# Two-layer product with GELU: W1 and W2 loaded in longer rows, and another order of the first two blocks

## The chip, the cores and the metric

The kernel runs on one core of a Trainium2 chip. The metric is the device time of one execution in microseconds (us), as a median over several runs. One more execution was recorded by the hardware profiler, and all durations below come from that one.

## The reference

```python
batch, m, k, h, n = 16, 512, 768, 3072, 768     # all float32
y = np.matmul(x, w1) + b1
y = 0.5 * y * (1.0 + erf(y / np.sqrt(2.0)))     # GELU
return np.matmul(y, w2).astype(np.float32)
```

x has 8192 rows in all. The kernel multiplies in 16-bit floats and adds up in 32 bits.

## The kernel before

**Seven products instead of eight.** The kernel takes the 8192 rows in eight blocks of 1024. In every block a matrix product is cut into two by two quarters, and the eight products of quarters are replaced by seven products of sums of quarters (the Winograd form of Strassen's method). The sums on the weight side are called T1 to T4, the raw quarters B11, B12, B21, B22; those on the x side are made by `x_sums` (L295), those on the hidden side by `g_sum`.

**First product.** A unit (`Unit1`) computes 128 hidden columns of the left half of W1 and 128 of the right half, for the two 512-row halves of the block: seven products `p1` to `p7` of three 128x512 matmuls each (L363). Twelve units make a block. Each unit needs one tile of W1: four raw quarters of 384 elements a partition, loaded and cast to 16 bits by GpSimd's DMA queue (`load_wt`, L186, DMAs on L195), and three more made of them by VectorE (`prep_wt`, L208; its operations are all recorded as L163). B12 is overwritten by T1. The finished tile of seven is also stored to DRAM by SyncE (`keep`, L205) for the blocks from 2 on.

**Second product.** For blocks 0 and 1 a unit (`Unit2`) computes 128 rows of each 512-row half with the same seven products, of twelve 128x384 matmuls each (L403). Blocks 2 to 7 use a second level of the method (`Unit3`, L455) on quarters of W2 which `split_w2` makes and stores to DRAM (L233) while blocks 0 and 1 run. The raw ones are stored as they lie; the computed ones pass through five staging buffers.

**Order.** The order on each engine is written out by hand. In a period (`period`, L577) TensorE does p1 of unit i, p7 of the unit j before it, p5 of i, p3 of j, p6 of i, p4 of j, p2 of i. Three PSUM steps hang on this: after p6 the sum is copied from bank bY to bank bZ (VectorE L570 or ACT L568), and p3 goes on there; p7 can only follow when that copy is done; VectorE then makes the two 32-bit sums c22 (L528) and c12 (L555), and ACT the GELU. Between the products `fill` puts VectorE's other work into the queues, by a budget in nanoseconds (`sums`), and DMAs at fixed points. Since engines work through their queues in order, an operation that waits for a transfer holds all that is queued behind it.

**The stretch around the change.** `seq` lists the 24 units of the first product of blocks 0 and 1; a unit's place in it is called its position. Block 0 goes first; block 1's x is loaded by GpSimd (`load_x`), transposed by SyncE's DMA queue (L283) into the layout the matmuls need, and summed on VectorE at the two positions ahead of block 1's first unit. Six slots hold W1 tiles: three of their own, three in the space of W2. A tile from number 6 on is loaded one position after block 1 has used the tile that lies in its slot. W2 is loaded (L214) in sixteen pieces of rows of 192 elements. At the turn from the first to the second product (`turn` in `period`) p1 of the first `Unit2` is spread between the last products of the last `Unit1`.

Of the kernel before, what the change touches and what calls it, by code (L numbers as in the profile page):

```python
# [10 lines left out]
P = 128  # L11
# [6 lines left out]
B11, B21, T1, B22, T3, T2, T4 = range(7)  # L18


@with_exitstack
def kernel(
# [24 lines left out]
    w2r = w2.rearrange("(hc p) n -> p hc n", p=P)  # L47
# [9 lines left out]
    w1s = [dp.tile([P, 7, KQ, P], F16, name=f"w1s{n}") for n in range(NH)]  # L57
# [56 lines left out]
    def wt_at(off):  # L114
        return cut(off, WT_N, "p (s k c) -> p s k c", s=7, k=KQ)
# [3 lines left out]
    wt_far = [wt_at(o_w2 + k * WT_N) for k in range(3)]  # L119
# [12 lines left out]
    def tmp_at(off):  # L132
# [8 lines left out]
    w2v = {slot: cut(off, W2_N, "p (h c n) -> p h c n", h=2, c=NH)  # L141
           for slot, off in ((B11, o_w2), (T3, o_w2 + W2_N), (T1, o_w2 + 2 * W2_N),
                             (B22, o_w2 + 3 * W2_N), (T2, o_x0),
                             (B21, o_x0 + W2_N + 2 * GS_N), (T4, o_x1 + XT_N))}
# [13 lines left out]
    with tc.manual_schedule():  # L158
# [27 lines left out]
        def load_wt(n):  # L186
            hi = hi_of(n)
            if n >= NH:
                wts[n] = wt_late[n % 4]
                nc.sync.dma_start(out=wts[n], in_=w1s[hi][:])  # L190
                return
            wts[n] = wt = wt_far[n - 3] if 3 <= n < 6 else wt_own[n % 3]
            for half in range(2):
                c0 = (half * NH + hi) * P
                nc.gpsimd.dma_start(  # L195
                    out=wt[:, 2 * half:2 * half + 2, :, :].rearrange("p a k c -> p (a k) c"),
                    in_=w1r[:, :, c0:c0 + P])

        def t_ops(o, n, q, ks=(0, 1, 2, 3)):

            for k in ks:
                d, a, b = ((T3, B22, T1), (T1, T1, B11), (T2, B22, T1), (T4, B21, T2))[k]
                later(n, lambda d=d, a=a, b=b: tt(o(d), o(a), o(b), SUB), q)
# [4 lines left out]
        def prep_wt(n):  # L208
            wt = wts[n]
            t_ops(lambda s: wt[:, s, :, :], KQ * P, soon)  # L210

        def load_w2(q, h, c):
            slot, r0, n0 = ((B11, 0, 0), (B21, NH, 0), (T1, 0, N2), (B22, NH, N2))[q]
            nc.gpsimd.dma_start(out=w2v[slot][:, h, c:c + NQ, :],  # L214
                                in_=w2r[:, r0 + c:r0 + c + NQ, n0 + h * N4:n0 + (h + 1) * N4])

        w2_parts = [(h, c) for c in (0, NQ) for h in range(2)]

        def prep_w2(h, c, q, ks):
            t_ops(lambda s: w2v[s][:, h, c:c + NQ, :], NQ * N4, q, ks)  # L220
# [125 lines left out]
        class Unit1:  # L346
# [11 lines left out]
            def mm(self, p, dst, first, c0, c1):  # L358
# [3 lines left out]
                for c in range(c0, c1):  # L362
                    nc.tensor.matmul(out=dst[:, 0:RH], lhsT=self.wt[:, slot, c, :],  # L363
# [13 lines left out]
            def right_done(self):  # L377
                hi = self.hi
                nc.scalar.activation(out=self.G[1][:, hi, :, :], in_=self.tmp, func=GELU,  # L379
                                     bias=b1t[:, NH + hi:NH + hi + 1])  # L380

            def left_done(self, row, bank):
                hi = self.hi
                nc.scalar.activation(out=self.G[0][:, hi, row, :], in_=bank[:, 0:RH], func=GELU,  # L384
                                     bias=b1t[:, hi:hi + 1])
# [175 lines left out]
        def p6(u):  # L561
            u.mm(6, bY[u.g % 2], False, 0, u.C)
            on_act = isinstance(u, Unit3) or (isinstance(u, Unit1) and u.sb > 0 and u.g % 2)
# [13 lines left out]
        def period(i, j, fill):  # L577

            turn = isinstance(j, Unit1) and not isinstance(i, Unit1)
            if turn and isinstance(i, Unit3):  # L580
# [16 lines left out]
            if turn:  # L597
                p7(j)
                fill(0)
                p1(i, 0, 5)  # L600
                p3(j)
                j.right_done()
                fill(0)
                p1(i, 5, 8)
                p4(j)
                p1(i, 8, i.C)
                copy_xy(i)
            else:
                if i and i.g:
                    p1(i, 0, i.C)  # L610
                    copy_xy(i)
                if j:
                    p7(j)
# [4 lines left out]
            if j and not turn:  # L618
# [4 lines left out]
            if j and not turn:  # L623
                j.right_done()
            fill(4)
            if j and not turn:
# [8 lines left out]
        wf = cut(GR + 8 * K, 8 * KQ * P).bitcast(FP32).rearrange(  # L635
            "p (h a c) -> p h a c", h=2, a=2 * KQ)
# [49 lines left out]
        for t in range(4, 8):  # L686
            if t == 6:
# [249 lines left out]
```

## Time and profile before

| | us |
|---|---|
| median of three runs | 882.42 |
| the three runs | 882.73, 877.61, 882.42 |
| the profiled execution | 877.73 |
| its span, first to last instruction | 876.0 |
| TensorE busy | 856.2 |
| VectorE busy | 650.2 |
| blocks 0 and 1, to the end of their second product | 248 |

A line of the timeline gives the start and the length in us, the engine, the line of the code, the operation, what it writes and reads, the shapes, how many were merged, and in brackets how long the engine stood idle before it and what it waited for. A line of the chain of waits gives start, length and what the execution was waiting on. A line of a DMA queue gives packets, MB and the time that the packets took as a share of the sixteen engines; a packet here is one row of a transfer, and times of packets overlap.

### The profile page before, as it was taken

How to read it: one execution, taken by the hardware profiler on the slowest of the kernel's cores; microseconds unless marked ns; L12 is line 12 of the kernel's file. 1: busy time of each engine (PE TensorE's matmuls, PEld its weight loads, DVE VectorE, ACT ScalarE, POOL GpSimd, SP SyncE). 2: the span in 40 equal slices, each digit the busy share in tenths (PEclk: the TensorE clock that was granted, in tenths of full speed). 3: DMA queues.
4: the chain of work that ended last, by engine and by line, in shares of the span. 5: the costliest groups of instructions: out<-in, count | busy, mean ns of one | idle time of the engine just before them, and what ended most of it. 6: DMA issues, size and time to landing. Idle time of an engine off the chain costs nothing.

```text
span 876.0 us, 16242 instructions
## 1 busy us (share of the span) xinstructions
PE 856.2 (98%) x6298; PEld 560.0 (64%) x6298; DVE 650.2 (74%) x1110; ACT 421.6 (48%) x686; POOL 95.4 (11%) x149
## 2 busy tenths in 40 slices
PE   8799999999999999999999999999999999999997
PEld 3344445666544599447984489744995459944697
DVE  5564577665546899578995799767997679956997
ACT  4577673111157712775128741477225771267511
POOL 6222210001100000200011000200002000010000
PEclk9999999999999999999999999999999999999999
DMA  9999683839969699996989969898898979967397
GB/s 215 177 268 187 108 174 118 327 146 243 243 200 299 180 320 346 255 292 198 325 323 263 291 224 321 291 287 208 286 329 278 309 168 309 350 225 262 104 295 275
DMA packets 155889, 219.42 MB, mean 250 GB/s; under 512 B 83532, under 2 KB 95236, under 8 KB 155812
## 3 DMA queue, kind: packets, MB, share of 16 engines
q1 hardware_dynamic: 112640, 181.01, 65.1%
q0 software_dynamic: 43136, 37.36, 23.0%
q8 instruction: 49, 0.80, 0.4%
q14 instruction: 28, 0.23, 0.1%
q10 hardware_dynamic: 36, 0.01, 0.0%
HBM read 180.30 MB, written 47.87 MB: 260 GB/s over the span
## 4 chain that ended last, share of the span: by engine, by line
PE 74%; DVE 13%; DMA 6%; issue 5%; POOL 1%; ACT 1%; SPq 0%; DVEq 0%; POOLq 0%; ACTq 0%
PE bY L363 17%; PE bX L363 11%; PE bY L455 10%; DVE arena L163 8%; PE bW L363 6%; PE bX L455 6%; PE bY L403 5%; PE bZ L363 5%; PE bX L403 4%; PE bZ L455 4%; PE bW L455 3%; DMA arena<-w1s 2%; PE bZ L403 2%; PE bW L403 2%; DMA arena<-in_w_dram 2%
## 5 line engine op out<-in xcount | busy, mean ns | idle before, releaser
L163 DVE TENSOR_TENSOR arena<-arena 128x768 f16<-128x768 f16 (+4 forms) x630 | 395.1, 656 | 18.6 <-DMA arena<-arena 8.0
L363 PEld LDWEIGHTS <-arena 128*128 128x128 f16 x2016 | 196.3, 98 | 245.1 <-issue 14.9
L455 PEld LDWEIGHTS <-arena 128*128 128x128 f16 x3528 | 292.1, 98 | 13.0 <-issue 4.5
L363 PE MATMUL bY<-arena 128*128 128x512 f16 x864 | 219.8, 380 | 7.9 <-DVE bZ L570 6.6
L528 DVE TENSOR_TENSOR arena<-bY,arena 128x512 f32<-128x512 f32 (+1 forms) x104 | 70.8, 681 | 160.1 <-PE bY L363 104.0
L363 PE MATMUL bX<-arena 128*128 128x512 f16 x576 | 141.8, 379 | 1.0 <-DMA arena<-w1s 1.0
L455 PE MATMUL bY<-arena 128*128 128x192 f16 x1512 | 139.8, 246 | 2.4 <-DVE bZ L565 2.4
L521 ACT COPY bY<-bX 128x512 f32<-128x512 f32 (+1 forms) x146 | 80.4, 550 | 127.5 <-DVE arena L497 90.8
L379 ACT ACTIVATE arena<-arena,b1t 128x1024 f16<-128x1024 f32 x96 | 110.3, 1149 | 60.5 <-DVE arena L555 60.5
L540 ACT COPY arena<-bW 128x512 f32<-128x512 f32 (+1 forms) x146 | 80.8, 553 | 93.4 <-PE bW L455 44.2
L403 PEld LDWEIGHTS <-arena 128*128 128x128 f16 x672 | 65.7, 98 | 44.2
L455 PE MATMUL bX<-arena 128*128 128x192 f16 x1008 | 92.0, 246 | 0.4
L555 DVE TENSOR_TENSOR arena<-bZ,arena 128x512 f32<-128x512 f32 (+1 forms) x104 | 70.5, 678 | 22.0 <-PE bZ L363 15.6
L363 PE MATMUL bW<-arena 128*128 128x512 f16 x288 | 78.5, 382 | 0.9 <-DVE arena L163 0.9
L363 PE MATMUL bZ<-arena 128*128 128x512 f16 x288 | 78.5, 382 | 0.0
L480 POOL DMA_DIRECT2D out_dram<-arena x42 | 30.1, 718 | 397.3 <-DVE arena L551 363.0
L384 ACT ACTIVATE arena<-bX,b1t 128x512 f16<-128x512 f32 x96 | 65.4, 681 | 7.9 <-PE bX L363 7.9
L384 ACT ACTIVATE arena<-bY,b1t 128x512 f16<-128x512 f32 x96 | 64.7, 674 | 0.0
L277 POOL DMA_DIRECT2D arena<-in_x_dram x60 | 32.4, 546 | 274.1 <-DMA arena<-arena 192.6
L568 ACT COPY bZ<-bY 128x512 f32<-128x512 f32 (+1 forms) x54 | 29.6, 548 | 52.9 <-DVE arena L555 36.3
L403 PE MATMUL bY<-arena 128*128 128x384 f16 x288 | 49.6, 326 | 0.0
L455 PE MATMUL bW<-arena 128*128 128x192 f16 x504 | 49.0, 246 | 0.1
(41 smaller groups left out, 359.7 us busy)
## 6 DMA issues: line engine op xcount, KB each, us to landing
arena<-w2s SPq DMA_DIRECT2D x294, 288.0 KB, 4.7
arena<-w1s SPq DMA_DIRECT2D x72, 672.0 KB, 6.5
out_dram<-arena POOLq DMA_DIRECT2D x42, 384.0 KB, 4.8
w2s<-arena SPq DMA_DIRECT2D x49, 288.0 KB, 3.9
arena<-in_x_dram POOLq DMA_DIRECT2D x60, 192.0 KB, 6.9
w1s<-arena SPq DMA_DIRECT2D x12, 672.0 KB, 5.2
out_dram<-arena SPq DMA_DIRECT2D x21, 384.0 KB, 3.2
arena<-in_w_dram POOLq DMA_DIRECT2D x16, 288.0 KB, 8.0
```

The source lines that it names most:

```text
L163: nc.vector.tensor_tensor(out=o, in0=a, in1=b, op=op)
L277: nc.gpsimd.dma_start(out=xhs[t], in_=xr[:, sb * 8 + t, :])
L363: nc.tensor.matmul(out=dst[:, 0:RH], lhsT=self.wt[:, slot, c, :], rhs=a[:, c, :], start=first and c == 0, stop=c == self.C - 1, skip_group ...
L379: nc.scalar.activation(out=self.G[1][:, hi, :, :], in_=self.tmp, func=GELU, bias=b1t[:, NH + hi:NH + hi + 1])
L384: nc.scalar.activation(out=self.G[0][:, hi, row, :], in_=bank[:, 0:RH], func=GELU, bias=b1t[:, hi:hi + 1])
L403: nc.tensor.matmul(out=dst[:, 0:N2], lhsT=a, rhs=w[:, :, c, :], start=first and c == 0, stop=c == self.C - 1, skip_group_check=True)
L455: nc.tensor.matmul(out=dst[:, t * N4:(t + 1) * N4], lhsT=a, rhs=w[:, c, :], start=first and c == 0 and t == 0, stop=c == NQ - 1, skip_grou ...
L480: eng.dma_start(out=orr[:, s0:s0 + 2, right * N2:(right + 1) * N2], in_=self.dst[:, r].rearrange("p t h n -> p t (h n)"))
L521: nc.scalar.copy(out=bY[u.g % 2][:, 0:u.F], in_=bX[u.g % 2][:, 0:u.F])
L528: nc.vector.tensor_tensor(out=u.c22(), in0=bY[u.g % 2][:, 0:u.F], in1=w[:, 0:u.F], op=ADD)
L540: nc.scalar.copy(out=w[:, 0:u.F], in_=bW[:, 0:u.F])
L555: nc.vector.tensor_tensor(out=u.c12(), in0=bZ[:, 0:u.F], in1=w[:, 0:u.F], op=ADD)
```

## The change

Unit k now takes columns 256k to 256k+127 as its left and 256k+128 to 256k+255 as its right part: the halves of W1 are made of alternating chunks of 128, and the rows of W2 and the bias are taken in the same alternation. A W1 tile is then one DMA of 1 KB rows, where it was two of 512 B rows. In the tile the four raw quarters lie interleaved (`w1_op` picks one out). W2 is loaded in nine DMAs of whole 3 KB rows, so B11 lies beside B12, and B21 beside B22; T1 gets a place of its own, and VectorE makes the sums three chunks at a time (`prep_w2`). There are seven slots for tiles. The list of units changes: seven of block 0 first, and the last of block 0 at position 17 instead of 20, six ahead of the end. The bZ copies of block 1 all go to VectorE (`sb >= ONE`, and ONE is 2). The special turn is removed.

```diff
 B11, B21, T1, B22, T3, T2, T4 = range(7)
+RAW = {B11: (0, 0), T1: (0, 1), B21: (1, 0), B22: (1, 1)}
...
     w1r = w1.rearrange("(kc p) c -> p kc c", p=P)
-    w2r = w2.rearrange("(hc p) n -> p hc n", p=P)
+    w2r = w2.rearrange("(hc s p) n -> p s hc n", s=2, p=P)
...
-    w1s = [dp.tile([P, 7, KQ, P], F16, name=f"w1s{n}") for n in range(NH)]
+    w1s = [dp.tile([P, 7 * KQ * P], F16, name=f"w1s{n}") for n in range(NH)]
     w2s = {(p, q): dp.tile([P, NQ, N4], F16, name=f"w2s{p}{q}")
...
     def wt_at(off):
-        return cut(off, WT_N, "p (s k c) -> p s k c", s=7, k=KQ)
+        return cut(off, WT_N)
+    def w1_raw(wt):
+        return wt[:, 0:4 * KQ * P].rearrange("p (k c) -> p k c", c=2 * P)
+    def w1_op(wt, slot):
+        raw = wt[:, 0:4 * KQ * P].rearrange("p (a k b c) -> p a b k c", a=2, k=KQ, b=2)
+        if slot in RAW:
+            return raw[:, RAW[slot][0], RAW[slot][1]]
+        return wt[:, slot * KQ * P:(slot + 1) * KQ * P].rearrange("p (k c) -> p k c", c=P)
...
     wt_own = [wt_at(o_wt + k * WT_N) for k in range(3)]
-    wt_far = [wt_at(o_w2 + k * WT_N) for k in range(3)]
+    W2P = 2 * W2_N
+    o_far = [o_w2 + W2P, o_w2 + W2P + WT_N, o_w2 + W2P + 2 * WT_N, o_w2 + W2P - WT_N]
+    slots = dict(enumerate([wt_at(o_wt + k * WT_N) for k in range(3)] + [wt_at(o) for o in o_far]))
+    slots.update({7: slots[0], 8: slots[1], 9: slots[2], 10: slots[3], 11: slots[4]})
     wt_late = [wt_at(o_wt2), wt_at(o_wt2 + WT_N)] + wt_own[:2]
...
              for k in range((o_x0 - o_stage) // WB)]
-    w2v = {slot: cut(off, W2_N, "p (h c n) -> p h c n", h=2, c=NH)
-           for slot, off in ((B11, o_w2), (T3, o_w2 + W2_N), (T1, o_w2 + 2 * W2_N),
-                             (B22, o_w2 + 3 * W2_N), (T2, o_x0),
-                             (B21, o_x0 + W2_N + 2 * GS_N), (T4, o_x1 + XT_N))}
+    w2rows = [cut(o_w2 + k * W2P, W2P, "p (c n) -> p c n", c=NH) for k in range(2)]
+    w2v = {}
+    for k, pair in enumerate(((B11, T3), (B21, B22))):
+        for m, slot in enumerate(pair):
+            w2v[slot] = w2rows[k][:, :, m * N2:(m + 1) * N2].rearrange("p c (h n) -> p h c n", h=2)
+    for slot, off in ((T2, o_x0), (T1, o_x0 + W2_N + 2 * GS_N), (T4, o_x1 + XT_N)):
+        w2v[slot] = cut(off, W2_N, "p (h c n) -> p h c n", h=2, c=NH)
     GS = [cut(o, GS_N, "p (c r) -> p c r", c=NH)
...
                 return
-            wts[n] = wt = wt_far[n - 3] if 3 <= n < 6 else wt_own[n % 3]
-            for half in range(2):
-                c0 = (half * NH + hi) * P
-                nc.gpsimd.dma_start(
-                    out=wt[:, 2 * half:2 * half + 2, :, :].rearrange("p a k c -> p (a k) c"),
-                    in_=w1r[:, :, c0:c0 + P])
-        def t_ops(o, n, q, ks=(0, 1, 2, 3)):
-            for k in ks:
-                d, a, b = ((T3, B22, T1), (T1, T1, B11), (T2, B22, T1), (T4, B21, T2))[k]
-                later(n, lambda d=d, a=a, b=b: tt(o(d), o(a), o(b), SUB), q)
+            wts[n] = slots[n]
+            nc.gpsimd.dma_start(out=w1_raw(wts[n]), in_=w1r[:, :, 2 * hi * P:2 * (hi + 1) * P])
...
         def prep_wt(n):
-            wt = wts[n]
-            t_ops(lambda s: wt[:, s, :, :], KQ * P, soon)
-        def load_w2(q, h, c):
-            slot, r0, n0 = ((B11, 0, 0), (B21, NH, 0), (T1, 0, N2), (B22, NH, N2))[q]
-            nc.gpsimd.dma_start(out=w2v[slot][:, h, c:c + NQ, :],
-                                in_=w2r[:, r0 + c:r0 + c + NQ, n0 + h * N4:n0 + (h + 1) * N4])
-        w2_parts = [(h, c) for c in (0, NQ) for h in range(2)]
-        def prep_w2(h, c, q, ks):
-            t_ops(lambda s: w2v[s][:, h, c:c + NQ, :], NQ * N4, q, ks)
+            o = {s: w1_op(wts[n], s) for s in range(7)}
+            for d, a, b in ((T3, B22, T1), (T1, T1, B11), (T2, B22, T1), (T4, B21, T2)):
+                later(KQ * P, lambda d=d, a=a, b=b: tt(o[d], o[a], o[b], SUB), soon)
+        def load_w2(k, c0, c1):
+            nc.gpsimd.dma_start(out=w2rows[k][:, c0:c1, :], in_=w2r[:, k, c0:c1, :])
+        W2C = 3
+        def prep_w2(d, c, q):
+            a, b = {T1: (T3, B11), T2: (B22, T1), T3: (B22, T3), T4: (B21, T2)}[d]
+            o = [w2v[s][:, :, c:c + W2C, :] for s in (d, a, b)]
+            later(2 * W2C * N4, lambda: tt(*o, SUB), q)
...
                 for c in range(c0, c1):
-                    nc.tensor.matmul(out=dst[:, 0:RH], lhsT=self.wt[:, slot, c, :],
+                    nc.tensor.matmul(out=dst[:, 0:RH], lhsT=w1_op(self.wt, slot)[:, c, :],
                                      rhs=a[:, c, :], start=first and c == 0,
...
                 nc.scalar.activation(out=self.G[1][:, hi, :, :], in_=self.tmp, func=GELU,
-                                     bias=b1t[:, NH + hi:NH + hi + 1])
+                                     bias=b1t[:, 2 * hi + 1:2 * hi + 2])
...
                 nc.scalar.activation(out=self.G[0][:, hi, row, :], in_=bank[:, 0:RH], func=GELU,
-                                     bias=b1t[:, hi:hi + 1])
+                                     bias=b1t[:, 2 * hi:2 * hi + 1])
...
             u.mm(6, bY[u.g % 2], False, 0, u.C)
-            on_act = isinstance(u, Unit3) or (isinstance(u, Unit1) and u.sb > 0 and u.g % 2)
+            on_act = isinstance(u, Unit3) or (isinstance(u, Unit1) and u.sb >= ONE and u.g % 2)
             if isinstance(u, Unit3) and u.add is not None:
...
-            turn = isinstance(j, Unit1) and not isinstance(i, Unit1)
-            if turn and isinstance(i, Unit3):
+            if isinstance(j, Unit1) and isinstance(i, Unit3):
                 p1(i, 0, i.C)
...
                 return
-            if turn:
-                p7(j)
-                fill(0)
-                p1(i, 0, 5)
-                p3(j)
-                j.right_done()
-                fill(0)
-                p1(i, 5, 8)
-                p4(j)
-                p1(i, 8, i.C)
+            if i and i.g:
+                p1(i, 0, i.C)
                 copy_xy(i)
-            else:
-                if i and i.g:
-                    p1(i, 0, i.C)
-                    copy_xy(i)
-                if j:
-                    p7(j)
+            if j:
+                p7(j)
             fill(1)
...
             fill(2)
-            if j and not turn:
+            if j:
                 p3(j)
...
                 p6(i)
-            if j and not turn:
+            if j:
                 j.right_done()
             fill(4)
-            if j and not turn:
+            if j:
                 p4(j)
...
         xf = cut(GR, 8 * K).bitcast(FP32).rearrange("p (t k) -> p t k", t=4)
-        wf = cut(GR + 8 * K, 8 * KQ * P).bitcast(FP32).rearrange(
-            "p (h a c) -> p h a c", h=2, a=2 * KQ)
+        wf = cut(GR + 8 * K, 8 * KQ * P).bitcast(FP32).rearrange("p (k c) -> p k c", c=2 * P)
         bf = cut(GR + 8 * K + 8 * KQ * P, 2 * P).bitcast(FP32)[0:2 * NH, :]
...
             nc.sync.dma_start(out=xf[:, t, :], in_=xr[:, t, :])
-        wts[0] = wt_own[0]
+        wts[0] = slots[0]
         for half in range(2):
-            c0 = half * NH * P
-            nc.sync.dma_start(out=wf[:, half], in_=w1r[:, :, c0:c0 + P])
+            r = slice(half * KQ, (half + 1) * KQ)
+            nc.sync.dma_start(out=wf[:, r, :], in_=w1r[:, r, 0:2 * P])
         nc.scalar.dma_start(out=bf, in_=b1.rearrange("(hc p) -> hc p", p=P))
...
             spin(2 if t < 3 else 6)
-        for half in range(2):
-            o = wts[0][:, 2 * half:2 * half + 2, :, :].rearrange("p a k c -> p (a k) c")
-            if half == 0:
-                nc.vector.tensor_copy(out=o, in_=wf[:, half])
-            else:
-                nc.scalar.copy(out=o, in_=wf[:, half])
+        nc.vector.tensor_copy(out=w1_raw(wts[0])[:, 0:KQ, :], in_=wf[:, 0:KQ, :])
+        nc.scalar.copy(out=w1_raw(wts[0])[:, KQ:2 * KQ, :], in_=wf[:, KQ:2 * KQ, :])
         prep_wt(0)
...
-        seq = ([(0, k) for k in range(6)] + [(1, 0), (1, 1), (1, 2), (0, 6), (1, 3), (1, 4), (0, 7),
-               (1, 5), (1, 6), (0, 8), (1, 7), (1, 8)] +
-               [(0, k) for k in range(9, NH)] + [(1, k) for k in range(9, NH)])
+        seq = ([(0, k) for k in range(7)] +
+               [(1, 0), (1, 1), (1, 2), (0, 7), (1, 3), (0, 8), (1, 4), (0, 9), (1, 6), (0, 10), (0, 11),
+                (1, 5), (1, 10), (1, 11), (1, 7), (1, 8), (1, 9)])
         at = {u: n for n, u in enumerate(seq)}
+        over = {7: 0, 8: 1, 9: 2, 10: 3, 11: 4}
...
-        w2_first = [(q, h, c) for h, c in w2_parts for q in (2, 3)]
+        w2_at_pos = {7: (0, 0, 2), 9: (0, 2, 4), 11: (0, 4, 6), 13: (0, 6, 8),
+                     at[1, 6] + 1: (0, 8, 10), at[1, 6] + 2: (0, 10, 12),
+                     at[1, 5] + 1: (1, 7, 12), at[1, 10] + 1: (1, 0, 3), at[1, 11] + 1: (1, 3, 7)}
...
             if pos == 0:
-                load_next_x(1, (0, 4))
                 load_wt(4)
-                load_next_x(1, (1, 5, 2))
+                load_next_x(1, (0, 4, 1, 5))
                 load_wt(5)
-                load_next_x(1, (6, 3, 7))
-            for n in range(6, NH - 1):
-                if pos == at[1, n - 3 if n >= 9 else n - 6] + 1:
+                load_next_x(1, (2, 6, 3, 7))
+                load_wt(6)
+            for n in range(7, NH):
+                if pos == at[1, over[n]] + 1:
                     load_wt(n)
-            if 4 <= pos < 12:
-                load_w2(*w2_first[pos - 4])
-            if pos in (12, 13):
-                for h, c in w2_parts[2 * pos - 24:2 * pos - 22]:
-                    load_w2(0, h, c)
-            if pos in (at[0, NH - 1] + 1, at[0, NH - 1] + 2):
-                for part in w2_parts[:2] if pos == at[0, NH - 1] + 1 else w2_parts[2:]:
-                    load_w2(1, *part)
+            if pos in w2_at_pos:
+                load_w2(*w2_at_pos[pos])
...
                     x_sums(1, soon, slice(h * RH // 2, (h + 1) * RH // 2))
-                if pos + 1 < len(seq) and seq[pos + 1][0] == 0 and pos != at[0, NH - 2]:
+                if pos + 1 < len(seq) and seq[pos + 1][0] == 0:
                     prep_wt(seq[pos + 1][1])
                 if pos == at[0, NH - 1] + 2:
-                    for c in (0, 6):
-                        for s in (0, 1):
-                            g_sum(s, 0, c, c + 6)
-                    for part in w2_parts:
-                        prep_w2(*part, queue, (2,))
-                        prep_w2(*part, late, (3,))
-                if pos == at[1, 8]:
-                    for part in w2_parts:
-                        prep_w2(*part, queue, (0, 1))
-            if slot == 3 and pos == at[0, NH - 2]:
-                prep_wt(NH - 1)
-            if pos >= 15:
+                    for c in range(0, NH, W2C):
+                        prep_w2(T1, c, queue)
+                    for k in (0, 1):
+                        g_sum(k, 0)
+                for m, c in ((21, 9), (22, 0), (23, 3), (23, 6)):
+                    if pos == m:
+                        prep_w2(T2, c, queue)
+                        prep_w2(T3, c, late if m == 23 else queue)
+                if pos == 23:
+                    for c in range(0, NH, W2C):
+                        prep_w2(T4, c, late)
+            if pos > at[0, NH - 1]:
                 if slot in (1, 4):
...
                 sums((0, 600, 300, 0, 600, 300)[slot])
-            if slot == 4:
-                if pos == at[0, NH - 3]:
-                    load_wt(NH - 1)
             if slot == 5:
...
             U = sb * NU + k
-            if slot == 0:
-                sums(1400)
-                return
             if slot == 1:
```

More of the change, by code (lines that the diff above doesn't have):

```diff
@@ L596, in period @@
                 return
-            if turn:
+            if i and i.g:
+                p1(i, 0, i.C)
+                copy_xy(i)
+            if j:
                 p7(j)
-                fill(0)
-                p1(i, 0, 5)
-                p3(j)
-                j.right_done()
-                fill(0)
-                p1(i, 5, 8)
-                p4(j)
-                p1(i, 8, i.C)
-                copy_xy(i)
-            else:
-                if i and i.g:
-                    p1(i, 0, i.C)
-                    copy_xy(i)
-                if j:
-                    p7(j)
             fill(1)
```

## The prediction

> **What bounds the kernel now.** I read the page first: TensorE is busy nearly everywhere, so a change of order can only win back time in which it waits or runs slowly.
>
> ```profile
> span 876.0 us, 16242 instructions
> ...
> PE 856.2 (98%) x6298; PEld 560.0 (64%) x6298; DVE 650.2 (74%) x1110; ACT 421.6 (48%) x686; POOL 95.4 (11%) x149
> ```
>
> The diff touches only blocks 0 and 1, which end at 248 us. So I took TensorE's timeline there. A period of the first product is seven products of three 128x512 matmuls; undisturbed, the double bX group (second product of a unit, then the first of the next) returns every 4.53 us (28.09, 32.63, 37.16). These lines show where it does not:
>
> ```profile
> 37.16 1.46 PE L363 MATMUL bX<-arena 128*128 128x512 f16 x6
> 43.33 1.44 PE L363 MATMUL bY<-arena 128*128 128x512 f16 x3 [4.72 <-DVE bZ L570]
> ...
> 48.86 1.46 PE L363 MATMUL bX<-arena 128*128 128x512 f16 x6
> ...
> 107.39 1.46 PE L363 MATMUL bY<-arena 128*128 128x512 f16 x6 [0.43 <-ACT bY L521]
> ...
> 111.56 0.81 PE L363 MATMUL bY<-arena 128*128 128x512 f16 x3 [1.42 <-DVE bZ L570]
> ...
> 134.89 0.81 PE L363 MATMUL bY<-arena 128*128 128x512 f16 x3 [0.45 <-ACT bZ L568]
> ...
> 138.78 2.12 PE L403 MATMUL bW<-arena 128*128 128x384 f16 x12
> ```
>
> From 37.16 to 48.86 is 11.70 us instead of 4.53: 7.17 lost, 4.72 of it idle, the rest slow matmuls (0.48 us apart after the pause, 0.22 before it). From 62.53 (position 9) to 129.09 (position 23) fourteen periods take 66.56 us instead of 63.42: 3.1 lost, most of it around 107 and 111. From 129.09 to the second product's 138.78 lie 0.65 + 7x0.648 + 3x0.648 + 1.95 = 9.08 us of matmuls: 0.6 lost. Sum 10.9 us.
>
> VectorE's timeline names the releasers, the chain of waits the transfer:
>
> ```profile
> 40.72 1.15 DVE L163 TENSOR_TENSOR arena<-arena 128x768 f16<-128x768 f16 x2 [5.19 <-DMA arena<-arena]
> ...
> 47.00 1.15 DVE L163 TENSOR_TENSOR arena<-arena 128x768 f16<-128x768 f16 x2 [0.74 <-DMA arena<-arena]
> ...
> 108.57 1.54 DVE L163 TENSOR_TENSOR arena<-arena 128x384 f16<-128x384 f16 x4 [2.10 <-DMA arena<-in_w_dram]
> ```
>
> ```profile
> 29.38 11.26 DMA arena<-arena
> ```
>
> VectorE's queue stood before the sums of block 1's x (L295) until four DMA transposes had landed at 40.63, so the bZ copy behind it (L570), and with it TensorE, was late. The other four landed at 46.9. At 108.5 the same happened with the last W1 tile (L186), loaded late into a reused slot.
>
> [...] from 30 to 31 us the two queues moved the same number of packets.
>
> ```profile
> q0 software_dynamic: 319, 0.08, 81.4%
> q1 hardware_dynamic: 320, 0.08, 67.6%
> ```
>
> [...] In the trace W1's packets (256 B written) run alone at 3544 in 5 us over 16 engines, 22.6 ns each; x's (1536 B) at 301 in 2 us, 106 ns: per source byte 0.044 against 0.035 ns, a fifth dearer, no more. [...] here 4.72 us idle were followed by doubled matmul times, while the 1.42 us at 111 were not. [...] strided 3x128 and contiguous 384 operands share one row here at 354 ns. So the new strides cost VectorE nothing.
>
> **The change, part by part.** *W1 in 1 KB rows.* A tile becomes one DMA of 768 packets (512 B written) instead of two of 768. Between W2's packets (384 B, 2026 in 4 us, 31.6 ns) and x's, the straight line gives 40 ns at 512 B: 1.94 us a tile instead of 2.17. Issue on POOL should be one 0.82 us instead of two. *Order at the start.* Ahead of block 1's first x now stands tile 4 (+1.94), against tiles 1 to 3 saving 0.7; x data, which landed first at 22.4, comes about 1 us later, but then the first four x stand together. In turns with one 256 B transpose packet a pair costs 50 ns beside W1 (320 a us), 133 beside x (243 in 2 us), I take 68 beside the new W1. From 27 us, when transposes start to pass: three x (384 packets, 3.2 us), tile 6 (3.3), the first W2 load (256 packets, 2.1) end near 36, and 1,400 of 6,144 transpose packets have passed. The rest runs at 1,010 a us (45 to 46 us) or at SP's own issue time, 1.3 us each and more: four transposes landed near 39, all near 43 to 45.
> *Block 1 starts one position later* (7, not 6), so its x sums stand one period later: VectorE reaches them at 39.98 and 45.7 us, after the landings. The 4.72 us and the half clock go. Next late is VectorE itself: position 5 holds four sums (0.57 each), four W1 preparations (0.37) and three steps of 0.61, 5.6 us in 4.53. Against the 0.5 us by which the bZ copy is early in a steady period, 0.6 us of TensorE wait remain.
> *Seven slots instead of six, loads a unit after a slot frees.* Tile 7 is wanted first: its single load now waits for all four raw products of (1,0), up to p3. Before, the second half of tile 6 waited for the same point, landed 3.85 us after issue and cost VectorE 0.37 us; a whole tile takes 0.85 more. The preparation, with the c12 sum (L555) and the bZ copy queued behind it, then starts 3.0 us into position 9 against 2.6: 0.2 us of TensorE wait, 0 to 0.8. Tiles 8 to 11 have a whole period more. The stalls at 107 to 112 go. Queued on POOL behind tile 7's wait are tile 8 and W2 loads, all with a period to spare.
> *W2 in 3 KB rows.* Rows 0 to 11 of one half stream in early. The others (1.97, 1.18, 1.57 MB) wait for units (1,5), (1,10), (1,11). At 106 ns a row: 640 rows 4.2 us, plus 2.75 us of issue and receipt (3.85 less 1.09) from 2.8 us into position 19: there 0.7 us into position 21, wanted at 2.2. The next two have 2.2 us and more. No wait, with 1.5 us of margin; a wait here stands before a bZ copy too.
> *The bZ copies of block 1's odd units go from ACT (0.58) to VectorE (0.61)*: 24 there instead of 18, six more in periods with 1 us or more of room; zero. Four W2 sums in position 19 (0.75 each) fill 4.8 us of 4.53 and use up the 0.5 us of slack.
> *The turn's interleaving goes*; G of block 0 and T1 are ready periods before, so the 0.6 us go.
> *Stores of raw W2 quarters* (twelve of 21, L233) now have 768 rows of 384 B instead of 128 of 2304 B. No row shows such stores. From below: 15.8 ns a row as the transposes' 256 B, 0.76 us each, as now (0.7). From above: the load's 31.6 ns doubled, an estimate, 3.0 us. I take 31.6, 1.5 us: ten microseconds more of DMA over 70 us in which SP waits for VectorE; zero.
> Left over: 0.6 + 0.2 + 0.2 (the small gap at 79.6, kept) + 0.2 for position 19 = 1.2 us. Gain 10.9 - 1.2 = 9.7. Span 876.0 to 866.3; that execution took 877.73 (1.7 around the span), so 868.0. It is the fast end of the runs (877.61, 882.42, 882.73), whose 5 us of scatter I have no cause for. The same 9.7 off their median: 872.7. Blocks 2 to 7 keep their instructions and shift.
>
> **The rivals.** *Half of it comes back as new waits (25%).* If SP's transposes keep their 3 us of issue each, the eighth lands near 46.5 and TensorE waits 2 us more at 47; tile 7 costs 0.8; the 640-row W2 load shares the engines with raw stores (133 ns a row, 1.1 us later), and each us past its margin stops TensorE. Together 4 to 6 less: 877.5. For it: both transfers were DMA-bound before. Against: the margins above.
> *It brings nothing (8%):* the early stall moves to position 6 whole, since loads and transposes are still the same bytes on the same engines, and only the 3 us around 107 to 112 and small things come and go: 881.
> *Slower (12%): the raw stores in SP's queue.* The nine for B11, B21 and B22 stand ahead of the first computed quarter; VectorE's sixth split operation needs one of five staging slots back. At 128 ns a row nine stores take 55 us and last until the second unit of the second product; VectorE stops 5 to 8 us there, and again for T3's three. Net +6: 888. It decides from about 100 ns a row; at 64 the backlog ends in time.
>
> **How the numbers follow.** Forecast as worked out: 55%, 868 to 876 by the scatter and the margins. A measurement of this kernel can tell about 1% from no change; 1% is 873.6, just above the forecast, so of its 55 points 45 fall below, and a few of the second case: faster 0.49, same 0.38, slower 0.13. The range goes from 866 (all 10.9 gone from the fastest run) to 882, which takes in the first two rivals.
>
> **What would show it.** Right: bX groups 4.53 us apart from position 1 to 23 but for a gap of 0.5 to 1 us near 47; the granted clock at 1.00 from 40 to 60 us (0.83 now); no VectorE wait on W1 over 1.2 us. Wrong: VectorE waiting for transposes beyond 1 us, for W2 in positions 21 to 23, or for its staging slots after 150 us.

## The result

Four runs of the changed kernel beside four of the kernel before, on one chip: 870.52 us median (869.06 to 871.25) against 880.01 (877.54 to 882.73), a ratio of 0.989 with a 95% interval of 0.985 to 0.993. The changed kernel is faster by about 9.5 us. The profiled execution took 871.2 us, 6.5 less than that of before (877.73).

The page of the changed kernel:

```profile
span 869.4 us, 16186 instructions
...
PE 853.5 (98%) x6298; PEld 560.2 (64%) x6298; DVE 653.0 (75%) x1114; ACT 418.9 (48%) x680; POOL 80.4 (9%) x131
...
q0 software_dynamic: 25184, 37.36, 20.4%
```

TensorE's work is the same; GpSimd's queue moves the same bytes in 25,184 packets, and moved them in 43,136 before. Read in the same way as before, by the bX groups of TensorE's timeline, which return every 4.53 us where nothing disturbs them:

```profile
40.50 1.46 PE L370 MATMUL bX<-arena 128*128 128x512 f16 x6
44.03 0.81 PE L370 MATMUL bY<-arena 128*128 128x512 f16 x3 [2.07 <-DVE bZ L577]
45.62 1.46 PE L370 MATMUL bW<-arena 128*128 128x512 f16 x3 [0.78 <-DVE arena L179]
...
49.73 1.46 PE L370 MATMUL bX<-arena 128*128 128x512 f16 x6
...
63.33 1.46 PE L370 MATMUL bX<-arena 128*128 128x512 f16 x6
...
69.08 1.46 PE L370 MATMUL bX<-arena 128*128 128x512 f16 x6
...
118.94 1.46 PE L370 MATMUL bX<-arena 128*128 128x512 f16 x6
...
124.70 1.46 PE L370 MATMUL bX<-arena 128*128 128x512 f16 x6
...
132.47 2.11 PE L410 MATMUL bW<-arena 128*128 128x384 f16 x12
```

Three periods are long: 40.50 to 49.73 by 4.70 us, 63.33 to 69.08 by 1.22, and 118.94 to 124.70 by 1.23. All others are 4.53. In what follows these are the losses of positions 5, 9 and 21: a loss is named by the position whose work on VectorE had to wait, and TensorE stops in the period after it, when it wants the bZ copy that is queued behind that work (it waited 2.07, 0.98 and 0.99 us for it). From 124.70 to the second product's 132.47 lie 7.77 us, only matmuls: the turn loses nothing. Together 7.15 us are lost where before 10.9 were. The long stretches after the two transfers of before, at 107 to 112 us, are gone; the early one is shorter; two of about 1.2 us are new.

VectorE's timeline names the releasers:

```profile
41.42 1.15 DVE L179 TENSOR_TENSOR arena<-arena 128x768 f16<-128x768 f16 x2 [2.55 <-DMA arena<-arena]
...
63.17 1.14 DVE L179 TENSOR_TENSOR arena<-arena 128x384 f16<-128x384 f16 x3 [1.47 <-DMA arena<-in_w_dram]
...
118.50 1.43 DVE L179 TENSOR_TENSOR arena<-arena 128x1152 f16<-128x1152 f16 x2 [1.20 <-DMA arena<-in_w_dram]
```

The shapes tell which transfer each was: 768 elements are the x sums, which wait for the fourth transpose; 384 are a W1 preparation, tile 7; 1152 are three chunks of W2, the load of five 3 KB rows a partition into the slots that unit (1,5) used.

So of the 6.6 us between the two spans (876.0, 869.4), 3.7 are lost time won back. The changed kernel's first bX group also came 1.2 us earlier (22.37 against 23.56), and block 2 began 5.0 us earlier (242.96 against 247.97). The last 1.6 us lie in blocks 2 to 7, whose instructions didn't change. This last part is scatter: in all ten profiles of this study blocks 2 to 7 took between 626.4 and 628.0 us, whichever kernel it was. The early start is taken up under runs 5 and 6.

### The profile page after: what moved, and what is told of

Its sections match the earlier page's. It is cut to its first block, busy times and chain, and to the rows that moved or that the text cites. A ratio compares the mean times of both kernels' runs of the same rounds, so it can differ in the third digit from the quotient of the medians.

```text
span 869.4 us, 16186 instructions
## 1 busy us (share of the span) xinstructions
PE 853.5 (98%) x6298; PEld 560.2 (64%) x6298; DVE 653.0 (75%) x1114; ACT 418.9 (48%) x680; POOL 80.4 (9%) x131
## 3 DMA queue, kind: packets, MB, share of 16 engines
q0 software_dynamic: 25184, 37.36, 20.4%
## 4 chain that ended last, share of the span: by engine, by line
PE 74%; DVE 14%; issue 6%; DMA 3%; ACT 1%; SPq 1%; POOL 0%; DVEq 0%; POOLq 0%
PE bY L370 17%; PE bX L370 11%; PE bY L462 10%; DVE arena L179 9%; PE bW L370 6%; PE bX L462 5%; PE bZ L370 5%; PE bY L410 5%; PE bX L410 4%; PE bZ L462 3%; PE bW L462 3%; PE bZ L410 2%; PE bW L410 2%; DMA arena<-in_w_dram 2%; DMA arena<-arena 1%
## 5 line engine op out<-in xcount | busy, mean ns | idle before, releaser
L179 DVE TENSOR_TENSOR arena<-arena 128x1536 f16<-128x1536 f16 (+6 forms) x628 | 393.8, 656 | 15.6 <-DMA arena<-arena 5.1
L577 DVE COPY bZ<-bY 128x512 f32<-128x512 f32 (+1 forms) x68 | 46.4, 682 | 6.3 <-PE bY L370 0.2
```

The lines of the kernel that those rows point to most:

```text
L179: nc.vector.tensor_tensor(out=o, in0=a, in1=b, op=op)
L577: nc.vector.tensor_copy(out=bZ[:, 0:u.F], in_=bY[u.g % 2][:, 0:u.F])
```

## The experiments

The kernel before was run beside them: 878.0 us median on the chip of the first four, 878.4 on that of the next three, 879.0 on that of the last. "Loss" is the time by which bX groups lie further apart than 4.53 us.

**1. The first W2 load one position later.** In the changed kernel the fourth transpose was late. Are the loads beside it the cause, or does SyncE need its time to issue transposes?

```diff
-        w2_at_pos = {7: (0, 0, 2), 9: (0, 2, 4), ...
+        w2_at_pos = {8: (0, 0, 2), 9: (0, 2, 4), ...
```

> The changed kernel with one thing moved: the first W2 load (256 rows of 3 KB) is put behind tile 7 in GpSimd's queue, so it no longer runs beside the transposes of block 1's x. My theory: position 5 loses 4.7 us of TensorE because x rows, tile 6 and this load take turns with the transposes; without it the first four transposes land about 2 us earlier than 41.3, VectorE's wait for them falls from 2.5 us to 0.5 or less, position 5 loses 1 to 2.5 us, and TensorE's clock is no longer halved there. Rival: SP's issue alone paces the transposes; then the landing stays at 41 and the loss at 4.7. Time: 2 to 3 us below the changed kernel by the theory, the same by the rival.

Measured: 868.19 us (867.08 to 868.96), ratio 0.989 (0.987 to 0.990). VectorE's and TensorE's timelines:

```profile
38.78 1.15 DVE L179 TENSOR_TENSOR arena<-arena 128x768 f16<-128x768 f16 x2 [0.24 <-DMA arena<-arena]
```

```profile
40.17 1.46 PE L370 MATMUL bX<-arena 128*128 128x512 f16 x6
...
45.58 1.46 PE L370 MATMUL bX<-arena 128*128 128x512 f16 x6
```

The sums waited 0.24 us instead of 2.55, and position 5 lost 0.88 instead of 4.70 (2.18 and 2.95 in two more profiles of the changed kernel, runs 5 and 6). One load of 2 rows a partition, queued where the transposes were finishing, was the cause of most of it; SyncE's issue was not the limit. Positions 9 and 21 kept 1.34 and 1.21.

**2. The same in the kernel before.** Is that early load the whole of the early loss there too?

```diff
-            if 4 <= pos < 12:
-                load_w2(*w2_first[pos - 4])
+            if 7 <= pos < 11:
+                for part in w2_first[2 * pos - 14:2 * pos - 12]:
+                    load_w2(*part)
```

> The kernel before with its first W2 loads put behind tile 6 in GpSimd's queue, nothing else. If transposes are late because they take turns with loads, the eighth transpose lands near 43 instead of 46.9 us and the fourth near 39.5 instead of 40.6; the loss around positions 4 to 6 falls from 7.2 to 5 or 6 us. If only the position at which block 1 starts matters (the later start in the changed kernel), the loss stays near 7. W2's later loads have several periods to spare in both cases.

Measured: 875.3 us (874.38 to 879.26), ratio 0.997 (0.995 to 0.999). TensorE's timeline:

```profile
36.49 1.46 PE L363 MATMUL bX<-arena 128*128 128x512 f16 x6
40.77 0.81 PE L363 MATMUL bY<-arena 128*128 128x512 f16 x3 [2.83 <-DVE bZ L570]
42.36 1.46 PE L363 MATMUL bW<-arena 128*128 128x512 f16 x3 [0.79 <-DVE arena L163]
```

The loss there was 5.43 us instead of 7.17: the fourth transpose landed at 38.1 us instead of 40.63 and VectorE didn't wait for the eighth, but block 1's sums are wanted one position, 4.5 us, sooner than in the changed kernel. So in the kernel before the load order is worth 1.7 us against this profile of it, 2.7 by the medians. The rest of the early loss stays. That it needs block 1's later start is argued and not shown: no run moves the start alone.

**3. The changed kernel with W1 in 512 B rows.** One part undone: the row length of W1, and with it two DMAs a tile where the changed kernel has one. The order, the slots and W2 stay as changed.

```diff
-            nc.gpsimd.dma_start(out=w1_raw(wts[n]), in_=w1r[:, :, 2 * hi * P:2 * (hi + 1) * P])
+            for b in range(2):
+                c0 = (2 * hi + b) * P
+                nc.gpsimd.dma_start(out=w1_raw(wts[n])[:, :, b * P:(b + 1) * P],
+                                    in_=w1r[:, :, c0:c0 + P])
```

> The changed kernel with W1 tiles after the first loaded as two DMAs of 512 B rows each, as in the kernel before; order, slots, W2 and the first tile stay. My theory: row length is worth little, 2.17 against 1.94 us a tile, and short rows let more transposes through in turn; position 5 loses about the same 4 to 5 us, tile 7 lands 0.3 us later; in all within 1 us of the changed kernel. Rival: the long rows are what the gain comes from; then 3 us or more are lost against the changed kernel, most of them before 60 us.

Measured: 873.17 us (871.41 to 874.67), ratio 0.994 (0.992 to 0.996). VectorE and TensorE:

```profile
43.74 1.15 DVE L179 TENSOR_TENSOR arena<-arena 128x768 f16<-128x768 f16 x2 [5.05 <-DMA arena<-arena]
```

```profile
46.35 1.44 PE L373 MATMUL bY<-arena 128*128 128x512 f16 x3 [4.58 <-DVE bZ L580]
```

The expectation fell. The early loss was 6.51 us, against 7.17 to 9.5 in the profiles with the loads of before, so by these profiles all that the change does besides the rows takes 0.7 to 3 us of it. It was as large as that because the loads passed longer beside the transposes: from 36 to 40 us 724 of their packets (0.44 MB) passed and 717 of the transposes', in the changed kernel 109 (0.14 MB) and 1,413, and the sums began at 43.74 us instead of 41.42. Another miss: tile 7 was not later. VectorE began its sums 2.97 us after the bX group of that period (63.39 and 60.42 us) without waiting for it, in the changed kernel 4.37 after (63.17 and 58.80) with 1.47 us of wait, and position 9 lost nothing. By the medians the long rows are worth about 3 us (873.2 against 870.1 and 870.5 for the changed kernel); by the early loss alone 2 to 4.

**4. Three moves that answer the three losses.** The W2 load later as in 1; unit (1,3) ahead of (0,7), so that tile 7 is wanted one position later; the W2 load after (1,5) in two, the three rows first that are wanted first.

```diff
-               [(1, 0), (1, 1), (1, 2), (0, 7), (1, 3), (0, 8), (1, 4), ...
+               [(1, 0), (1, 1), (1, 2), (1, 3), (0, 7), (0, 8), (1, 4), ...
-        w2_at_pos = {7: (0, 0, 2), 9: (0, 2, 4), ...
+        w2_at_pos = {8: (0, 0, 2), 9: (0, 2, 4), ...
-                     at[1, 5] + 1: (1, 7, 12), ...
+                     at[1, 5] + 1: (1, 9, 12), ...
+            if pos == at[1, 5] + 1:
+                load_w2(1, 7, 9)
```

> The changed kernel with three moves: the first W2 load behind tile 7; unit (0,7) one position later, after (1,3); and the last W2 rows of the second half loaded as rows 9 to 11 first, then 7 and 8. Theory: each of the three losses left in the changed kernel has the cause that the trace names: position 5 (4.7 us) falls to 1 to 2.5, position 9 (1.2 us, tile 7 landing 1.5 us after VectorE asks for it) to 0, position 21 (1.2 us, W2 load landing 1.2 us after VectorE asks) to 0. Span about 865 against 869.4. Rival: waits move on to the next transfer and the sum stays above 5 us, span 868 or more.

Measured: 865.3 us (864.92 to 868.5), ratio 0.986 (0.984 to 0.988), the fastest kernel of the study. TensorE's timeline:

```profile
40.55 1.46 PE L370 MATMUL bX<-arena 128*128 128x512 f16 x6
...
43.03 0.82 PE L370 MATMUL bW<-arena 128*128 128x512 f16 x3 [0.37 <-DVE arena L179]
...
45.63 1.46 PE L370 MATMUL bX<-arena 128*128 128x512 f16 x6
```

Of the first product's periods only this one is long, by 0.55 us, and its only wait is for VectorE's own work: the overload of position 5 that the prediction put at 0.6. The waits at positions 9 and 21 are gone.

**5 and 6. How much is scatter?** The changed kernel again, and the changed kernel with the first tile, which SyncE loads in 1 KB rows, back in 512 B rows. The second asks whether the 1.2 us by which the first bX group came earlier belong to the change.

```diff
-            r = slice(half * KQ, (half + 1) * KQ)
-            nc.sync.dma_start(out=wf[:, r, :], in_=w1r[:, r, 0:2 * P])
+            r = slice(half * P, (half + 1) * P)
+            nc.sync.dma_start(out=wf[:, :, r], in_=w1r[:, :, r])
...
```

(Left out: the casts of the two halves, which follow the same slices.)

> The changed kernel itself, beside the kernel before on the same chip. The loss at position 5 is a race of transfers against VectorE, so it may vary by a microsecond or two; the ratio should stay between 0.985 and 0.993, and blocks 2 to 7 should take 626 to 628.5 us as in every kernel so far.

> The changed kernel with the first W1 tile loaded by SP as before: two DMAs of 512 B rows by column half. In the profiles so far TensorE passes position 1 at 22.0 to 22.4 us with 1 KB rows in the first tile and at 22.9 and 23.6 with 512 B rows. Theory: the rows of the first tile are worth 0.5 to 1.2 us, so position 1 is passed at 22.8 or later here and the span grows by about that. Rival: the start varies by itself; then 22.0 to 22.4 and no change.

Measured: 870.13 us (869.23 to 871.78), ratio 0.991 (0.988 to 0.994), and 870.08 (868.86 to 871.58), ratio 0.991 (0.988 to 0.993). The first bX group came at 23.34 us with long rows and at 22.50 with short ones, so the rows of the first tile don't set the start. It isn't wholly settled: over all profiles the group came at 22.89 to 23.56 in the four with the loads of before, and at 22.04 to 22.50 in five of the six others. Up to 0.8 us, the difference of the two means, may belong to the change.

The losses of the changed kernel vary too: 2.18, 0.95 and 0.86 us in the second profile, 2.95, 1.16 and 0.99 in the third. VectorE's waits for the fourth transpose, in run 5 and in run 6, show where the largest comes from:

```profile
41.38 1.15 DVE L179 TENSOR_TENSOR arena<-arena 128x768 f16<-128x768 f16 x2 [1.54 <-DMA arena<-arena]
```

```profile
41.31 1.15 DVE L179 TENSOR_TENSOR arena<-arena 128x768 f16<-128x768 f16 x2 [2.31 <-DMA arena<-arena]
```

In all three profiles the sums began at 41.3 to 41.4 us. What differs is when VectorE came to them: 38.87, 39.84 and 39.00 us, each 16.5 us after the first bX group. A start that is 1 us earlier is only waited away here. The rest of the difference is TensorE's clock: in the third profile its matmuls kept their 0.22 us after nearly the same idle time,

```profile
43.92 0.81 PE L370 MATMUL bY<-arena 128*128 128x512 f16 x3 [1.83 <-DVE bZ L577]
45.51 0.82 PE L370 MATMUL bW<-arena 128*128 128x512 f16 x3 [0.78 <-DVE arena L179]
```

where in the first those of 45.62 us took 0.42, at a granted clock of 0.79 from 42 to 50 us.

**7. The kernel before without the turn.** The special order at the turn taken out, alone.

```diff
-            turn = isinstance(j, Unit1) and not isinstance(i, Unit1)
+            turn = isinstance(j, Unit1) and isinstance(i, Unit3)
```

> The kernel before with the special turn alone removed, so that the last unit of the first product and the first of the second are interleaved as any two units. In the kernel before, VectorE runs six sums of 0.75 us without a pause there, from 137.8 us, for the first products of the second part. Theory: with block 0 ending only three positions ahead, these sums are not ready for the plain order, and removing the turn costs 1 to 4 us of TensorE; the changed kernel can do without it because block 0 ends six ahead. Rival: the turn was only a cost of 0.6 us, and the kernel gets faster by that.

In this kernel VectorE writes T4 of W2 over x sums that p3 of the last unit of block 1 still has to read, so that unit computes other values. Measured: 880.09 us (878.27 to 882.86), ratio 1.002 (1.001 to 1.003). TensorE's timeline:

```profile
138.79 2.11 PE L403 MATMUL bW<-arena 128*128 128x384 f16 x12
142.87 0.81 PE L363 MATMUL bZ<-arena 128*128 128x512 f16 x3 [1.97 <-DVE arena L163]
```

There is a wait at the turn, as expected, but it is p3's for that T4, not the wait for sums that the theory had named. So this run doesn't tell the two apart, and another was made.

**8. The same, with T4 held back** until p3 is issued, as it was in the kernel before.

```diff
-            if slot == 2:
+            if slot == (3 if U == 0 else 2):
                 soon.extend(late)
                 late.clear()
+            if slot == 2:
                 if U + 1 < 2 * NU:
```

> The kernel before without the turned order at the end of block 1, the x sums of the last unit held back to slot 3 so that they stay ahead of the fourth step's transform: one part of the change alone, without its half tiles of W1 and its 3 KB rows of W2. Theory of the prediction: the kernel before needs the turn because its first product of block 0 ends only 3 units ahead of block 1's first, so without it the end of block 1 waits for sums by VectorE: a wait of 0.5 us or more between the last units of block 1 and block 2's first, and the time 0.5 to 2 us above the kernel before, ratio 1.000 to 1.002. Rival: the turn's 0.6 us is saved just as well without the rest of the change; no wait there, the last unit of block 1 takes 0.6 us less than in the kernel before, ratio 0.9985 to 1.000. Early stalls stay as in the kernel before in both (5 to 10 us near 36 to 50 us, by chance).

Measured: 877.56 us (875.72 to 882.64), ratio 0.999 (0.997 to 1.000). TensorE's timeline:

```profile
130.18 1.46 PE L363 MATMUL bX<-arena 128*128 128x512 f16 x6
...
137.95 2.11 PE L403 MATMUL bW<-arena 128*128 128x384 f16 x12
```

7.77 us, the same as in the changed kernel, and no wait. In the kernel before it was 9.69 us from the same group, at 129.09, of which the prediction counts 9.08 as matmuls. The rival holds: the turn's order cost 0.6 us in the kernel before, and could go without any other part of the change, if T4 is held back. The ratio agrees with 0.6 us but is too coarse to show it; the trace does. The early loss in this profile was 8.42 us, and 9.5 in that of run 7, with the same loads as before: it varies from one profile to the next between at least 7.2 and 9.5.

**All profiles together.** What is lost in blocks 0 and 1 up to the second product, and the span less that loss:

| | early | later W1, W2 | turn | span | span less losses |
|---|---|---|---|---|---|
| before | 7.17 | 3.1 | 0.6 | 876.0 | 865.1 |
| before, W2 behind (2) | 5.43 | 3.2 | 0.6 | 872.6 | 863.4 |
| before, no turn (7) | 9.5 | 3.2 | 2.0 | 878.3 | 863.6 |
| before, no turn, T4 later (8) | 8.42 | 3.1 | 0 | 876.2 | 864.6 |
| changed | 4.70 | 2.45 | 0 | 869.4 | 862.3 |
| changed again (5) | 2.18 | 1.81 | 0 | 867.4 | 863.4 |
| changed, first tile (6) | 2.95 | 2.15 | 0 | 868.3 | 863.2 |
| changed, W2 behind (1) | 0.88 | 2.55 | 0 | 866.4 | 863.0 |
| changed, 512 B rows (3) | 6.51 | 1.16 | 0 | 871.1 | 863.4 |
| three moves (4) | 0.55 | 0 | 0 | 863.1 | 862.6 |

The last column differs by under 3 us while the spans differ by 15, so nearly all that the change did to the time is in the losses. The profiled execution of before has the highest rest, that of the changed kernel the lowest; the 2.8 us between these two are the start and the scatter named under the result. The mean of the rest is 864.2 us in the first four rows and 863.0 in the others. Most of that 1.2 us is the earlier start.

## Why the prediction was right or wrong

**The total.** Forecast was 872.7 us from a median of 882.42, a ratio of 0.989; measured were 0.989 and, on another chip, 0.991. The profiled pair won 6.5 us where 9.7 were forecast. Losses of 1.2 us were to be left over; 7.15, 3.99 and 5.10 were left in three profiles of the changed kernel. Part of that is made good because the profile of before, on which the sum was made, was on the low side for the early loss: 7.17, where runs 7 and 8 with the same loads had 9.5 and 8.42. With the mean of the three, 12.1 us in all were lost before and 5.4 after, 6.7 less. The medians differ by 9.5 and 8.2; of the 1.5 to 3 us between, up to 0.8 may be the start, and for the rest, which lies inside the intervals, I have no cause. So the ratio came out partly by luck: 4.2 us more were left than forecast, and more had been lost before than the one profile showed. By the waits that were left, the rival "half of it comes back as new waits" was right: it put them at 4 to 6 us and named tile 7 and the W2 load behind unit (1,5), which both came. It was the fourth transpose, though, and not the eighth that was late. By the total, the forecast was right.

The signs that the prediction named for itself say the same. VectorE waited 2.55 us for transposes, where more than 1 was to mean "wrong"; 1.20 us for W2 at position 21, where any wait was; and 1.47 us for W1, where 1.2 was the limit. Only the wait for staging slots never came.

**Which losses go: right.** The stalls at 107 to 112 us went wholly. They did in run 3 too, so the long rows of W1 are not needed for it; whether the seventh slot or the new order of units did it, no run separates. The turn's 0.6 us went; run 8 shows that it needed no more than T4 held back. The early loss went in part.

**W1 in 1 KB rows: right in its price, wrong in its weight.** 1.94 us a tile were forecast; tiles landed 2.0 us apart. By 36 us about 1,390 transpose packets had passed (forecast 1,400), and a pair of a transpose packet and a new W1 packet took 68 ns as assumed: from 32 to 33 us the two queues moved 235 and 234, so in turn here too. VectorE's operations of 384 elements, on the interleaved tiles, took 353 ns, those of before 354. (Two slips of the working change nothing: 40 ns a packet give 1.92 us a tile, and 0.044 against 0.035 ns is a quarter dearer, not a fifth.) What I had not seen is how much hangs on it. In run 3, with short rows, 724 load packets still passed from 36 to 40 us instead of 109, and most of the early loss is back.

**"The rest runs at 1,010 a us ... four transposes landed near 39": the step that failed.** The loads were to end near 36 us; the first W2 load landed at 38.97. These two views of the changed kernel's DMA queues, each a window of 40 slices, show what the transposes did meanwhile. The digits are the busy share of sixteen engines in tenths:

```profile
DMA  9998995929999990909191919999999129001001
GB/s 249 195 181 160 215 82 51 68 34 55 85 58 79 61 72 3 181 3 68 24 44 10 68 24 202 240 266 280 263 276 41 24 27 14 7 7 10 7 7 10
...
q1 hardware_dynamic: 1038, 0.26, 133.2%
q0 software_dynamic: 13, 0.02, 3.1%
```

```profile
DMA  9999119110010004993999999999999999999999
GB/s 266 270 277 123 27 24 21 7 10 7 7 10 7 7 7 102 280 75 72 280 294 251 280 297 294 283 290 300 280 294 254 277 297 294 280 294 300 280 283 280
```

The first is 37 to 40 us, the second 39 to 42. The loads are nearly done (13 packets of theirs are left), yet the transposes pass at 1,038 in 3 us, 346 a us. There are two slow stretches: 37.4 to 38.8 us, at some 60 GB/s, while the last load packets pass, and 39.5 to 40.1, at 7 to 10 GB/s and a busy share below two tenths, mostly below one. Then, after one more dip, 280 GB/s, the rate that the prediction had assumed throughout (1,010 packets of 256 B a us are 260). The fourth transpose landed at 41.33 instead of 39.

In run 1, with one load less at this point, it landed at 38.69. From 36 to 40 us not one load packet passes there, and the second stretch is there all the same, from 37.8 to 38.4:

```profile
DMA  9679999999999999950010006999999999999999
GB/s 166 33 172 292 265 289 284 287 289 292 287 339 276 274 274 282 131 20 8 8 10 8 8 8 138 289 260 294 287 287 289 292 287 234 248 233 220 225 212 210
```

Run 2 has one as well, at 8 GB/s from 37.1 to 37.8 us. So it is not what the load costs, and the forecast would have had to count it in any case. What the load changes is when the full rate comes: run 1 moved 33 GB/s at 36.1 us and 265 to 339 from 36.3 to 37.6, where the changed kernel was at some 60 from 37.4 to 38.8. That the loads' place sets the landing was tested by runs 1 and 2, their row length by run 3. Why the transposes fall to 8 GB/s, and why they slow down beside so few load packets, stays open.

**Half clock.** I expected the granted clock at 1.00 from 40 to 60 us; it was 0.91, and 0.79 from 42 to 50. Here 2.07 us idle, three matmuls and 0.78 us idle were followed by matmuls of 0.42 us instead of 0.22 (three from 45.62 to 46.87, granted clock 0.50 from 46 to 47), as were 2.83 and 0.79 in run 2; 1.83 and 0.78 in run 6 and 1.06 and 0.78 in run 5, at the same place, were not. So an idle stretch as long as the 4.72 us of before is not needed; what decides between 2.07 and 1.83 us, no trace here shows. VectorE's waits of 2.55, 2.31 and 1.54 us for the transposes thus cost 4.70, 2.95 and 2.18 us of TensorE's time: by these numbers some 1.5 us of the 4.70 are the clock, an estimate.

VectorE also came to the sums at 38.87 us instead of the forecast 39.98, because the first bX group came 1.2 us earlier. So of the 2.55 us of wait 1.1 are the early start; the late landing used up the margin of 1 us and made the rest.

**VectorE at position 5: right.** 0.6 us forecast, 0.55 in run 4, where nothing else stands there.

**Tile 7: the right mechanism, too small.** 0.2 us forecast, 1.22, 0.95 and 1.16 measured. The sum itself held a slip: 2.63 us and 0.85 for the other half are 3.5, not 3.0. The rest is the landing, 4.95 us after the issue; the tile was ready 3.7 us into position 9.

**W2 in 3 KB rows: no wait forecast, 1.23, 0.86 and 0.99 measured.** The step that failed is the start, "from 2.8 us into position 19". The load overwrites the whole slot of unit (1,5), T sums included, and so waits for p4, the last product to read it, not for p3: it was issued at 110.34 us, 4.35 into the position. It landed 8.14 us after, against the 6.95 of the sum: alone, from 114 to 117 us, 131 to 135 of its packets passed a us, some 120 ns each where 106 were taken, which makes 0.6 us; the rest lies at its beginning, where from 112 to 113 us 36 of its packets passed beside 130 of the raw stores, the sharing that the rival had named. Run 4 takes away the wait by loading first the three rows that are wanted first.

**The bZ copies on VectorE: zero, right.** From position 2 on TensorE waits for bZ (L577) only where VectorE itself waited for a transfer just before (2.07, 0.98 and 0.99 us).

**Raw stores in 384 B rows: right.** Between 128 and 130 us the changed kernel's stores have the engines to themselves:

```profile
DMA packets 1631, 0.61 MB, mean 307 GB/s; under 512 B 1631, under 2 KB 1631, under 8 KB 1631
```

2 us times 16 engines by 1631 are 19.6 ns a row, 0.94 us a quarter, under the 31.6 ns taken. The 2304 B rows of before ran at 385 GB/s from 136 to 138 us, so the short rows cost a fifth of the rate. "Slower" would have needed 100 ns a row by the forecast's estimate, and nothing waits for a staging slot. What they hold back is the W2 load above, for about half a microsecond, an estimate from its 8.14 us of landing against the sum's 6.95 and the 0.6 of its longer rows' time.

## What to carry to other kernels

Where an engine waits for a DMA, look at what other queues move in its last microseconds, not at its own length alone, and move what can wait behind it (run 1: one load moved, the fourth transpose 2.6 us sooner). When a load overwrites a slot, find the last reader of all that it overwrites, not of the part that it replaces first (here the load after unit (1,5) was issued 4.35 us into its position instead of 2.8). And make the sum of losses by period on more than one profile: here the largest loss varied from 7.2 to 9.5 us with the loads of the kernel before and from 2.2 to 4.7 in the changed one.

## What was not expected of the hardware

Three things. In the changed kernel and in runs 1 and 2 the transposes fell once to some 8 GB/s for 0.6 to 0.8 us, with no load packet beside them; the cause was not found. TensorE's clock was halved (granted 0.50, matmuls of 0.42 us instead of 0.22) after 2.07 and 0.78 us of idle time with three matmuls between them, and not after 1.83 and 0.78. And one DMA of 768 rows for tile 7, landed 4.95 us after its issue, made VectorE wait 1.47 us, where in run 3 it came as two of half the bytes and VectorE didn't wait; yet tiles of one DMA landed 2.0 us apart, where the forecast had 2.17 for a tile of two.
